# The rest of a rounded weight in plain products: from a VectorE subtraction to an accumulating transfer from GpSimd's queue

## The chip, the cores and the metric

One core of a Trainium2 chip runs the whole program in one launch. The metric is the device time of one execution in microseconds (us); the kernel before takes 2423.59 us, the median of three runs (2423.26 to 2424.36).

## The reference

Two layers of a diffusion backbone on 640 tokens (512 latent tokens, 128 of context) of width 1024. Each layer has a SwiGLU feed-forward block, a mixer (pooling, windowed attention and an order-2 Hyena convolution side by side) and a second feed-forward block, each with a normed and modulated input and a gated residual:

```python
def swiglu(h, wg, wu, wd):
    return (jax.nn.silu(h @ wg) * (h @ wu)) @ wd
...
    h = rmsnorm(x, p['norm'][0]) * (1 + sc1) + sh1
    x = x + 0.5 * g1 * swiglu(h, p['wg'][0], p['wu'][0], p['wd'][0])
    h = rmsnorm(x, p['norm'][1]) * (1 + sc2) + sh2
    u = h @ p['w_in']
...
    mix = jnp.concatenate([y_pool, a, y_hy], axis=-1) @ p['w_out']
    x = x + g2 * mix
```

All inputs are fp32, the feed-forward width is 2816, and w_in, w_out and the three feed-forward matrices are the weights this document speaks of.

## The kernel before, in words

Activations lie with the width on the partitions, 640 tokens in two halves of 320 (`HT`). fp32 products are made of three products of rounded operands: every operand is held as a part `hi`, rounded to the type fp32r, and a rest `lo`, and PE computes hi·hi, hi·lo and lo·hi (`mul`, L331). `split` makes the two: a cast on ACT (L295) and a subtraction on VectorE (L296). Activations are named ahi/alo or hhi/hlo, weights whi/wlo or kwh/kwl.

Weights come from DRAM in blocks of 128 x 512 or 128 x 384 through SP's queue into `raw`, one of `RAWB` = 4 buffers. Three users split them:

- `load_weight` (L298) for plain products: whi and wlo in `WB` = 5 buffers each. `gemm` (L337) takes one block after another and multiplies it with both halves, 24 matmuls for 512 columns. This serves some gate and up columns, the most of the down products and the mixer's products.
- `load_keep` (L312) for products whose weights are used twice, first for half 0 and then for half 1, so that a norm can follow half by half: kwh and kwl in slots of a common pool. It serves the tail of each of three feed-forward blocks (`DNSKEW` = 5 output columns of the down product, two blocks of 512 and 384 alternating, ten blocks a tail), the start of the feed-forward blocks (gate and up of `UPSKEW` = 2 columns), the start of a mixer (w_in, `MIXSKEW` = 4) and its output (w_out).
- `Seven` (L577), Winograd's form of seven products for the other gate and up columns, has its own `part` (L591), which calls `split` on sums of blocks.

Each engine issues in the order that a scheduler has set at build time from priorities and its own costs. Weight loads and their splits get a higher priority by `AHEAD` = 150 and `AHK` = 150, so they stand ahead of the products that take them, as far as buffers allow. The norm's chain passes over several engines: squares on ACT (`sq`, L453) summed on VectorE (L455), a sum over partitions on PE (`tot`), the variance on VectorE (`var`, L480), its power -1/2 on POOL (`rs`, L482), a diagonal matrix on VectorE (`dg`, L499) and its broadcast by PE (`rsb`). VectorE also computes the modulation vectors from big tables (`junk`, L410), 240 instructions in the gaps. POOL does little else than `rs` and some masks.

Of the kernel before, what the change touches and what calls it, by code (L numbers as in the profile page):

```python
# [11 lines left out]
F32 = mybir.dt.float32  # L12
# [3 lines left out]
ALU = mybir.AluOpType  # L16

P = 128
# [64 lines left out]
def make_consts():  # L83
# [22 lines left out]
    def parts(t):  # L106
        """Two parts of few bits each along a new axis after the partitions."""
        t = t.astype(np.float32)
        m, e = np.frexp(t)
        high = np.ldexp(np.round(m * 4096.0) / 4096.0, e).astype(np.float32)  # L110
        return np.stack([high, t - high], axis=1).reshape(P, 512)
# [19 lines left out]
    for ch in range(2):  # L131
        for half in range(2):
            w = (2, 4, 8, 16)[ch * 2 + half]
            rows = slice(64 * half, 64 * half + 64)
# [49 lines left out]
def hybrid_kernel(ctx: ExitStack, tc: tile.TileContext, a, depth=2, fc=22):  # L184
    nc = tc.nc
    V, S, G, DMA = nc.vector, nc.scalar, nc.gpsimd, nc.sync

    class PE:
        """The tensor engine; while fixed is set it issues in the order of this program."""
        last, fixed = None, False  # L190
# [74 lines left out]
    def load_tables(name, h, n, new=slot):  # L265
        """Tables of cosines and sines, each as the two parts that reduced products take."""
        ts = []
        for q in range(n):
            t = new(512, F32R, name="tab")
            DMA.dma_start(out=t.bitcast(F32), in_=a[name][h, q])  # L270
            ts.append(t.rearrange("p (h c f) -> p h c f", h=2, c=2))
        return ts

    def triple(ps, l_, r_, start, stop):
        """One product from three of parts: left and right are pairs of a rounded operand and its rest."""
        for n, (lh, rh) in enumerate(((l_[0], r_[0]), (l_[0], r_[1]), (l_[1], r_[0]))):
            PE.matmul(out=ps, lhsT=lh, rhs=rh, start=(start and n == 0), stop=(stop and n == 2))
# [16 lines left out]
    def split(src, hi, lo):  # L294
        S.copy(out=hi, in_=src)  # L295
        V.tensor_tensor(out=lo, in0=src, in1=hi.bitcast(F32), op=ALU.subtract)  # L296

    def load_weight(src, n):  # L298
        with tc.high_priority(offset=min(AHEAD, tc.cur_priority)):
            raw = wp.tile([P, n], F32, tag="raw", bufs=RAWB, name=nm("raw"))  # L300
            DMA.dma_start(out=raw, in_=src)
            hi = wp.tile([P, n], F32R, tag="whi", bufs=WB, name=nm("whi"))
            lo = wp.tile([P, n], F32R, tag="wlo", bufs=WB, name=nm("wlo"))
            split(raw, hi, lo)
        return hi, lo
# [6 lines left out]
    def load_keep(src, ahead=AHK):  # L312
        out = []
        for k0, k1 in groups(src.shape[-1] // P, 5):
            n = (k1 - k0) * P
            hi, lo = slot(n, F32R, "kwh"), slot(n, F32R, "kwl")
            with tc.high_priority(offset=min(ahead, tc.cur_priority)):
              for j0, j1 in groups(k1 - k0, 4):
                raw = wp.tile([P, (j1 - j0) * P], F32, tag="raw", bufs=RAWB, name=nm("raw"))
                DMA.dma_start(out=raw, in_=src[:, (k0 + j0) * P:(k0 + j1) * P])  # L320
                split(raw, hi[:, j0 * P:j1 * P], lo[:, j0 * P:j1 * P])
            out.append((k0, k1, (hi, lo)))
        return out
# [36 lines left out]

# [1 line left out]
    condT = cp.tile([P, DC, 32], F32, name="condT")  # L362
# [34 lines left out]
    def ada_group(l, g):  # L397
        """Modulation vectors as products of rows of the transposed weights with the condition, summed along them."""
        def load(n):
            raw = wp.tile([P, 1024], F32, tag="araw", bufs=ARAWB, name=nm("araw"))  # L400
            DMA.dma_start(out=raw, in_=a["adat"][l * 9 + g - len(AG0), n])
            ada_raw[l, g, n] = raw

        def step(n):
            raw = ada_raw[l, g, n // 2]
            i, r = n // 2, n % 2
            c, s = i // 2, i % 2
            junk = tp.tile([P, 1024], BF16, tag="junk", bufs=1, name=nm("junk"))
            with tc.issue_after(pace[0]) if pace else nullcontext():
                V.tensor_tensor_reduce(out=junk, in0=raw, in1=condb[:, r], scale=1.0, scalar=bias(l, g)[:, s, c, r:r + 1],  # L410
                                       op0=ALU.mult, op1=ALU.add, accum_out=mods[l][:, g, c, s, r:r + 1])
            if n == 2 * DC - 1:
                done.add((l, g))

        for n in range(2 * DC):
            ada_q.append(((lambda n=n: load(n // 2)) if n % 2 == 0 else None, lambda n=n: step(n)))
# [27 lines left out]

# [1 line left out]
    ssq = [None, None]  # L446
# [11 lines left out]
    class Norm:  # L458
# [77 lines left out]
        def twist(self):  # L536
            """Sums of the quarters of the normed input that the seven products take; yields after each block of rows."""
            B = modv(self.key[0], self.key[2])
# [36 lines left out]

# [1 line left out]
    class Seven:  # L577
        """Gate and up columns of one block as seven products of sums of quarters (Winograd's form of Strassen's
        scheme): rows are gate and up, columns the two halves of the tokens, the inner dimension is cut in the middle."""

# [213 lines left out]

# [1 line left out]
    filt = {}  # L796
# [6 lines left out]
    def sine(ps, n, q, outs):  # L803
        """Both layers at once, one in each half of the partitions."""
        aa, k = slot(n, name="sa"), slot(n, name="sk")
# [60 lines left out]
    class Filter:  # L866
        """The spectra of one layer's filters of one order."""
        W = 256
# [7 lines left out]
        def pair(self, win, src, c0, first=False):  # L876
            """Taps of the forward and the backward filter, their sum and difference, and their magnitudes."""
            w = slot3(1, self.W, name="win")
# [78 lines left out]

# [1 line left out]
    def cmul(z, k, o, prime):  # L959
# [193 lines left out]

# [1 line left out]
    NAMES = ORDER  # L1155
    def mixer(l, cur, nxt):
# [182 lines left out]
        blocks = []  # L1339
# [39 lines left out]
        def stage_a(j):  # L1379
            """Scores and softmax of the two heads that share a query tile; yields after each block of queries."""  # L1380
            qhi, qlo = qhl[j]
            m = [tiny(4, "m", 8) for _ in range(2)]
            ss = [[], []]
            for b in range(4):
                wi, k0, k1, msk, mo, kbs = blocks[b]
# [8 lines left out]
                for kv in range(2):  # L1394
                    s = slot(512, name="sc")
# [138 lines left out]
        def last():  # L1534
            """The first output blocks' products, but for the query tile that comes last."""
            kept.extend(load_keep(a["wout"][l, d, :, 512:1024]) for d in range(4))
            yield
            for d in range(4):
                open_[d] = acc()
                mul(open_[d], kept[d][0][2], 0, 3, 4, ahl, 0)  # L1540
                yield
# [30 lines left out]

# [1 line left out]
    DMA.dma_start(out=craw, in_=a["cond"])  # L1574
# [230 lines left out]
```

## Time and profile before

| | before |
|---|---|
| median of 3 runs | 2423.59 us |
| span of the profiled execution | 2421.6 us |
| PE busy | 2369.5 us, 98% |
| VectorE (DVE) busy | 1922.5 us, 79% |
| ScalarE (ACT) busy | 1096.9 us, 45% |
| GpSimd (POOL) busy | 18.7 us, 1%, 46 instructions |
| hardware DMA queue | 267.75 MB, 34.7% of 16 engines |

The span is that of one execution taken by the profiler, from the first instruction to the last; the metric is some 2.0 us longer. An engine's share is an average over the whole span: a stage can be bound by another engine than the one with the largest share. PE, DVE, ACT, POOL and SP are the engines; PEld is PE's loading of weights and SPq the queue that issues transfers. PEclk is the granted clock of PE, 1.00 being full speed. A name such as kwl<-raw,kwh gives the output and the inputs of an instruction, L296 the line of the kernel.

### The profile page before, as it was taken

What the parts mean: (1) busy time and instruction counts of PE and PEld (TensorE: products, weight loads), DVE (VectorE), ACT (ScalarE), POOL (GpSimd) and SP (SyncE); (2) the same over time, 40 slices, a digit from 0 to 9 for tenths busy, and PEclk for the clock granted to TensorE, in tenths of its full rate; (3) what the DMA queues carried; (4) which work ended last, traced back from release to release, by engine and by line L of the source; (5) the groups of instructions that cost most, each with busy time, mean ns of one, the idle gap of its engine ahead of it and who ended that gap; (6) DMA issues with size and microseconds to landing.
All of it is one profiled execution on the core that took longest, in us unless ns stands there. A gap on an engine that the chain in (4) does not pass through costs nothing.

```text
span 2421.6 us, 41063 instructions
## 1 busy us (share of the span) xinstructions
PE 2369.5 (98%) x15576; PEld 2243.7 (93%) x15576; DVE 1922.5 (79%) x3885; ACT 1096.9 (45%) x2228; POOL 18.7 (1%) x46
## 2 busy tenths in 40 slices
PE   8999999999989999999999999999998999999999
PEld 3799999999877999999999999999987789999999
DVE  7888898858887897998858778785888788567583
ACT  4653353533445553443536435253434556335251
POOL 0000000000000000000000000000000000000000
PEclk9999999999999999999999999999998999999999
DMA  9434444324411334344322433432441122222222
GB/s 330 160 110 136 135 123 156 99 81 158 135 44 43 103 120 142 127 133 150 101 72 95 127 122 108 133 113 84 135 132 63 47 88 77 81 84 78 84 68 90
DMA packets 132645, 270.36 MB, mean 112 GB/s; under 512 B 15002, under 2 KB 24924, under 8 KB 132320
## 3 DMA queue, kind: packets, MB, share of 16 engines
q1 hardware_dynamic: 132448, 267.75, 34.7%
q8 instruction: 122, 2.00, 0.3%
q14 instruction: 75, 0.61, 0.1%
HBM read 259.56 MB, written 8.13 MB: 111 GB/s over the span
## 4 chain that ended last, share of the span: by engine, by line
PE 92%; DVE 4%; issue 1%; ACT 1%; DMA 1%; POOL 0%; SPq 0%; POOLq 0%; DVEq 0%; ACTq 0%
PE mm L205 78%; PE Z L205 5%; PE o L205 1%; PE pt L209 1%; PE yt L205 1%; PE fk L205 1%; PE mx L205 1%; PE ada L205 1%; PE zf L205 1%; DVE junk L410 0%; PE rsb L205 0%; PE pm L205 0%; PE qbc L205 0%; POOL rs L482 0%; DMA ar<-in_ada 0%
## 5 line engine op out<-in xcount | busy, mean ns | idle before, releaser
L295 ACT CAST whi<-raw 128x512 fp32r<-128x512 f32 (+1 forms) x394 | 238.9, 607 | 467.8 <-PE mm L205 432.8
L205 PE MATMUL mm<-hhi,whi 128*128 128x320 f32 x1440 | 447.6, 311 | 2.9 <-ACT u L1218 2.9
L205 PE MATMUL mm<-hhi,wlo 128*128 128x320 f32 x1440 | 445.7, 310 | 0.0
L205 PE MATMUL mm<-hlo,whi 128*128 128x320 f32 x1440 | 445.3, 309 | 0.0
L205 PE MATMUL mm<-ahi,whi 128*128 128x320 f32 x1198 | 370.2, 309 | 0.0
L205 PE MATMUL mm<-alo,whi 128*128 128x320 f32 x1198 | 370.2, 309 | 0.0
L205 PE MATMUL mm<-ahi,wlo 128*128 128x320 f32 x1198 | 370.2, 309 | 0.0
L296 DVE TENSOR_TENSOR wlo<-raw,whi 128x512 fp32r<-128x512 f32 (+1 forms) x394 | 263.0, 671 | 80.8 <-ACT whi L295 78.7
L410 DVE CUSTOM_DVE_ANT_0 junk<-araw,condb,par 128x1024 bf16<-128x1024 f32 x240 | 307.1, 1280 | 5.2 <-DMA araw<-in_adat 4.1
L205 PEld LDWEIGHTS mm<-hhi,whi 128*128 128x128 f32 x1440 | 270.4, 188 | 7.7 <-ACT u L1218 4.5
L205 PEld LDWEIGHTS mm<-hhi,wlo 128*128 128x128 f32 x1440 | 270.5, 188 | 2.3 <-issue 2.3
L205 PEld LDWEIGHTS mm<-hlo,whi 128*128 128x128 f32 x1440 | 270.3, 188 | 1.0 <-issue 0.9
L205 PE MATMUL mm<-thi,whi 128*128 128x320 f32 x864 | 267.0, 309 | 0.0
L205 PE MATMUL mm<-tlo,whi 128*128 128x320 f32 x864 | 267.0, 309 | 0.0
L205 PE MATMUL mm<-thi,wlo 128*128 128x320 f32 x864 | 267.0, 309 | 0.0
L205 PEld LDWEIGHTS mm<-ahi,wlo 128*128 128x128 f32 x1198 | 224.9, 188 | 0.0
L205 PEld LDWEIGHTS mm<-alo,whi 128*128 128x128 f32 x1198 | 224.9, 188 | 0.0
L205 PEld LDWEIGHTS mm<-ahi,whi 128*128 128x128 f32 x1198 | 224.9, 188 | 0.0
L295 ACT CAST whi<-ex 128x512 fp32r<-128x512 f32 x216 | 134.3, 622 | 188.9 <-PE mm L205 177.6
L296 DVE TENSOR_TENSOR wlo<-ex,whi 128x512 fp32r<-128x512 f32 x216 | 149.0, 690 | 34.8 <-ACT whi L295 30.3
L295 ACT CAST whi<-ws 128x512 fp32r<-128x512 f32 x144 | 89.4, 621 | 163.2 <-PE mm L205 124.0
L205 PEld LDWEIGHTS mm<-thi,whi 128*128 128x128 f32 x864 | 162.2, 188 | 0.0
(263 smaller groups left out, 4710.8 us busy)
## 6 DMA issues: line engine op xcount, KB each, us to landing
araw<-in_adat SPq DMA_DIRECT2D x120, 512.0 KB, 3.8
raw<-in_wgu SPq DMA_DIRECT2D x208, 256.0 KB, 2.9
ex<-in_wgu SPq DMA_DIRECT2D x144, 256.0 KB, 2.7
raw<-in_wd SPq DMA_DIRECT2D x128, 256.0 KB, 2.7
raw<-in_win SPq DMA_DIRECT2D x56, 256.0 KB, 3.2
ar<-in_ada SPq DMA_DIRECT2D x48, 256.0 KB, 5.5
raw<-in_wd SPq DMA_DIRECT2D x64, 192.0 KB, 2.5
tab<-in_tfi SPq DMA_DIRECT2D x32, 256.0 KB, 4.1
```

The lines of the kernel that those rows point to most:

```text
L205: cls.order(nc.tensor.matmul(**k))
L209: cls.order(nc.tensor.transpose(**k))
L295: S.copy(out=hi, in_=src)
L296: V.tensor_tensor(out=lo, in0=src, in1=hi.bitcast(F32), op=ALU.subtract)
L410: V.tensor_tensor_reduce(out=junk, in0=raw, in1=condb[:, r], scale=1.0, scalar=bias(l, g)[:, s, c, r:r + 1], op0=ALU.mult, op1=ALU.add, ac ...
```

## The change

Blocks that `load_weight` and `load_keep` load are no longer split by `split` but by a new helper. The cast on ACT stays; a second instruction on ACT writes the negated rounded part into lo; and a transfer from the queue of POOL adds the weights, read once more from DRAM, onto it. `raw` is then read by the cast alone. `Seven` and all splits of activations stay as they were.

```diff
+    def split_weight(src, raw, hi, lo):
+
+        S.copy(out=hi, in_=raw)
+        S.mul(out=lo, in_=hi.bitcast(F32), mul=-1.0)
+        G.dma_start(out=lo, in_=src, accum_op=ALU.add)
...
     def load_weight(src, n):
...
-            split(raw, hi, lo)
+            split_weight(src, raw, hi, lo)
...
     def load_keep(src, ahead=AHK):
...
-                split(raw, hi[:, j0 * P:j1 * P], lo[:, j0 * P:j1 * P])
+                split_weight(src[:, (k0 + j0) * P:(k0 + j1) * P], raw, hi[:, j0 * P:j1 * P], lo[:, j0 * P:j1 * P])
```

Apart from this only docstrings and comments are gone, so that a line after the helper stands six lines lower (L482 is L488). The list of POOL grows from 51 to 395 rows: 344 transfers, 280 of 256 KB and 64 of 192 KB, 86 MB together. VectorE's list falls by 344 rows and ACT's grows by 344. PE's has the same products in a partly different order.

ACT at the first tail (sq are the squares of the columns before, kwh and kwl the kept blocks of the down weights), before:

```order
L453 ACTIVATE sq_5702<-x 128x320
L295 CAST kwh_5705<-raw_5707 128x512
L295 CAST kwh_5711<-raw_5713 128x384
L295 CAST kwh_5717<-raw_5719 128x512
L295 CAST kwh_5723<-raw_5725 128x384
```

and with the change:

```order
L459 ACTIVATE sq_5756<-x 128x320
L300 CAST kwh_5759<-raw_5761 128x512
L301 ACTIVATE kwl_5760<-kwh_5759 128x512
L300 CAST kwh_5766<-raw_5768 128x384
L301 ACTIVATE kwl_5767<-kwh_5766 128x384
L300 CAST kwh_5773<-raw_5775 128x512
L301 ACTIVATE kwl_5774<-kwh_5773 128x512
```

Each cast is now followed by the negated copy of the same block. PE at the same tail, before:

```order
L205 MATMUL mm_5789<-ahi_4696,kwh_5705 128x320 [waits DVE_49,Activation_49]
L205 MATMUL mm_5789<-alo_4697,kwh_5705 128x320
L205 MATMUL mm_5789<-ahi_4696,kwl_5706 128x320 [waits DVE_49]
L205 MATMUL mm_5789<-ahi_4849,kwh_5705 128x320
L205 MATMUL mm_5789<-alo_4850,kwh_5705 128x320
```

and with the change:

```order
L205 MATMUL mm_5857<-ahi_4744,kwh_5759 128x320 [waits DVE_49,Activation_49]
L205 MATMUL mm_5857<-alo_4745,kwh_5759 128x320
L205 MATMUL mm_5883<-ahi_4744,kwh_5773 128x320 [waits DVE_49,PE_49,Activation_49]
L205 MATMUL mm_5883<-alo_4745,kwh_5773 128x320
L205 MATMUL mm_5857<-ahi_4744,kwl_5760 128x320 [waits DMASW6_49]
```

Two products of the next output column are put ahead of the first one that takes a kwl, which now waits on a transfer.

PE at the second feed-forward start (831 us in the trace; hhi and hlo are the normed input, kwh and kwl the kept gate and up weights, tot and rsb the norm's steps), before:

```order
L205 MATMUL tot_9268<-ones,sq_9213 128x1 [waits DVE_49]
L205 MATMUL tot_9268<-ones,sq_9213 128x1 x2
L205 MATMUL mm_9276<-hhi_9140,kwl_8904 128x320
L205 MATMUL mm_9362<-hhi_9102,kwh_9217 128x320 [waits Activation_49]
L205 MATMUL mm_9362<-hlo_9103,kwh_9217 128x320
L205 MATMUL mm_9362<-hhi_9102,kwl_9218 128x320 [waits DVE_49]
L205 MATMUL mm_9362<-hhi_9108,kwh_9217 128x320
L205 MATMUL mm_9362<-hlo_9109,kwh_9217 128x320
L205 MATMUL mm_9362<-hhi_9108,kwl_9218 128x320
L205 MATMUL rsb_9301<-dg_9302,ones 128x128 [waits DVE_49]
```

and with the change:

```order
L205 MATMUL tot_9384<-ones,sq_9325 128x1 [waits DVE_49]
L205 MATMUL tot_9384<-ones,sq_9325 128x1 x2
L205 MATMUL mm_9392<-hhi_9252,kwl_9015 128x320
L205 MATMUL mm_9478<-hhi_9214,kwh_9329 128x320 [waits Activation_49]
L205 MATMUL mm_9478<-hlo_9215,kwh_9329 128x320
L205 MATMUL rsb_9417<-dg_9418,ones 128x128 [waits DVE_49]
L205 MATMUL rsb_9417<-dg_9421,ones 128x128 [waits DVE_49]
L205 MATMUL rsb_9417<-dg_9424,ones 128x64 [waits DVE_49]
L205 MATMUL mm_9503<-hhi_9214,kwh_9343 128x320 [waits PE_49,Activation_49]
L205 MATMUL mm_9503<-hlo_9215,kwh_9343 128x320
L205 MATMUL mm_9531<-hhi_9214,kwh_8993 128x320 [waits Activation_49]
L205 MATMUL mm_9478<-hhi_9214,kwl_9330 128x320 [waits DMASW0_49]
```

The three rsb and three first products of other weights now stand ahead of the first product that takes the new kwl, which waits on a transfer (DMASW0) in place of VectorE.

POOL at the same place with the change; before, its list had the two rs alone there:

```order
L302 DMA kwl_9008<-in_wgu 128x512
L302 DMA kwl_9015<-in_wgu 128x512
L488 TENSOR_TENSOR rs_9160<-var_9158,mhalf 128x3
L488 TENSOR_TENSOR rs_9390<-var_9388,mhalf 128x3
L302 DMA kwl_9330<-in_wgu 128x512
L302 DMA kwl_9337<-in_wgu 128x512
L302 DMA kwl_9344<-in_wgu 128x512
L302 DMA kwl_9351<-in_wgu 128x512
```

The transfers into the last four kept gate and up blocks stand behind both rs of the norm in POOL's list, the first four ahead of them.

PE at the first mixer output (785 us; ahi and alo are the mixer's results, kwh and kwl the kept w_out, pt and o belong to the attention), before:

```order
L205 MATMUL mm_8775<-ahi_8215,kwh_8751 128x320 [waits Activation_49]
L205 MATMUL mm_8775<-alo_8216,kwh_8751 128x320
L205 MATMUL o_8726<-pt_8744,va_6433 64x256
L205 MATMUL mm_8775<-ahi_8215,kwl_8752 128x320 [waits DVE_49]
L205 MATMUL mm_8775<-ahi_8431,kwh_8751 128x320
```

and with the change:

```order
L205 MATMUL mm_8879<-ahi_8311,kwh_8851 128x320 [waits Activation_49]
L205 MATMUL mm_8879<-alo_8312,kwh_8851 128x320
L205 MATMUL o_8826<-pt_8844,va_6505 64x256
L205 MATMUL o_8826<-pt_8849,va_6505 64x256
L209 MATMUL pt_8905<-ident,sc_8595 128x128 [waits PE_49]
L209 MATMUL pt_8905<-ident,sc_8621 128x128
L209 MATMUL pt_8905<-ident,sc_8647 128x128
L205 MATMUL mm_8917<-ahi_8311,kwh_8858 128x320 [waits Activation_49]
L205 MATMUL mm_8917<-alo_8312,kwh_8858 128x320
L205 MATMUL mm_8927<-ahi_8311,kwh_8865 128x320 [waits Activation_49]
L205 MATMUL mm_8927<-alo_8312,kwh_8865 128x320
L205 MATMUL mm_8879<-ahi_8311,kwl_8852 128x320 [waits DMASW4_49]
```

One o, three pt and four products of two later blocks are moved ahead of the first product that takes a kwl.

## Rows read from the trace of the kernel before

**Rows 1.** The page, parts 1 and 3 (DMA: packets, MB, share).
```profile
PE 2369.5 (98%) x15576; PEld 2243.7 (93%) x15576; DVE 1922.5 (79%) x3885; ACT 1096.9 (45%) x2228; POOL 18.7 (1%) x46
...
q1 hardware_dynamic: 132448, 267.75, 34.7%
```

**Rows 2.** PE's waits: line waited for: us in total, times, longest us.
```profile
PE pt L209 <- DVE sc L1351: 7.6, 4, 3.6
PE mm L205 <- ACT kwh L295: 5.8, 3, 2.0
...
PE yt L205 <- DVE cy L969: 2.1, 1, 2.1
...
PE mm L205 <- DVE hlo L533: 1.8, 4, 0.5
PE mm L205 <- DVE kwl L296: 1.7, 4, 0.7
```

**Rows 3.** Timeline, first tail: start us, us, instruction, count [idle before <-releaser].
```profile
509.96 1.16 DVE L296 TENSOR_TENSOR kwl<-raw,kwh 128x512 fp32r<-128x512 f32 x2
...
510.71 0.42 PE L205 MATMUL mm<-ahi,kwl 128*128 128x320 f32 x1 [0.17 <-DVE kwl L296]
```

**Rows 4.** Timeline, first mixer output, VectorE and PE.
```profile
785.51 0.69 DVE L296 TENSOR_TENSOR kwl<-raw,kwh 128x512 fp32r<-128x512 f32 x1 [0.37 <-ACT kwh L295]
...
787.15 0.41 PE L205 MATMUL mm<-ahi,kwl 128*128 128x320 f32 x1
```

**Rows 5.** Timeline, first mixer start, ACT and PE.
```profile
548.24 0.60 ACT L295 CAST kwh<-raw 128x512 fp32r<-128x512 f32 x1
...
553.83 0.41 PE L205 MATMUL mm<-hhi,kwl 128*128 128x320 f32 x1 [0.66 <-DVE kwl L296]
```

**Rows 6.** Timeline, first start of the down products, ACT and PE.
```profile
204.32 0.63 ACT L295 CAST whi<-raw 128x512 fp32r<-128x512 f32 x1
...
211.60 0.31 PE L205 MATMUL mm<-ahi,wlo 128*128 128x320 f32 x1
```

**Rows 7.** Timeline of POOL at the three feed-forward starts.
```profile
831.24 0.85 POOL L482 TENSOR_TENSOR rs<-var,mhalf 128x3 f32<-128x3 f32 x1 [17.99 <-DVE var L480]
...
1269.17 1.24 POOL L482 TENSOR_TENSOR rs<-var,mhalf 128x3 f32<-128x3 f32 x1 [15.48 <-DVE var L480]
...
1990.18 0.85 POOL L482 TENSOR_TENSOR rs<-var,mhalf 128x3 f32<-128x3 f32 x1 [17.97 <-DVE var L480]
```

**Rows 8.** Timeline of PE at the same three places.
```profile
831.34 0.31 PE L205 MATMUL mm<-hhi,kwl 128*128 128x320 f32 x1
...
1271.03 0.39 PE L205 MATMUL mm<-hhi,kwl 128*128 128x320 f32 x1
...
1990.14 0.31 PE L205 MATMUL mm<-hlo,kwh 128*128 128x320 f32 x1
1990.29 0.31 PE L205 MATMUL mm<-hhi,kwl 128*128 128x320 f32 x1
```

**Rows 9.** Groups by shape: count | busy us, mean ns | idle before.
```profile
L295 ACT CAST kwh<-raw 128x512 fp32r<-128x512 f32 x79 | 46.3, 621 | 29.4 <-DMA raw<-in_wd 14.7 <-DMA raw<-in_wgu 9.1 <-DMA raw<-in_win 5.3
...
L410 DVE CUSTOM_DVE_ANT_0 junk<-araw,condb,par 128x1024 bf16<-128x1024 f32 x240 | 307.1, 1280 | 5.2 <-DMA araw<-in_adat 4.1
L296 DVE TENSOR_TENSOR wlo<-raw,whi 128x512 fp32r<-128x512 f32 x345 | 235.7, 687 | 40.8 <-ACT whi L295 39.0
```

**Rows 10.** The page, part 6: DMA issues, count, KB each, us to landing.
```profile
raw<-in_wd SPq DMA_DIRECT2D x128, 256.0 KB, 2.7
...
ar<-in_ada SPq DMA_DIRECT2D x48, 256.0 KB, 5.5
```

**Rows 11.** Windows: us, engines' busy us, PEclk, DMA share, GB/s.
```profile
507.70:509.98 2.28, 0.33 (x4) 0.07 (x2) 1.59 (x5) 1.14 (x4) 0.00 (x0) 1.00 0.00 0
511.60:515.08 3.48, 3.48 (x15) 3.48 (x14) 0.59 (x2) 1.03 (x2) 0.00 (x0) 0.51 0.82 243
711.70:716.40 4.70, 4.68 (x11) 3.11 (x12) 4.70 (x10) 2.52 (x6) 0.00 (x0) 0.50 0.01 3
```

## Prediction

> **What bounds the kernel now.** I first read the busy shares at the head of the page [rows 1]: TensorE is busy for 98% of the span of 2421.6 us, VectorE for 79%. So VectorE's work counts only where PE waits for it, and the change must be judged at the places where PE takes a fresh weight. The profiled execution's 2421.6 us stand beside a median of 2423.59 us; the sum is made against the former, and 2.0 us are added at the end.
>
> Second, PE's waits [rows 2]. The subtraction that the change removes (kwl, L296) held PE up four times, for 1.7 us in all. That is the direct gain at most. Behind the four is the question that decides: how long before PE's first use of a rest is its cast done? I call this the lead. In the steady run of plain products it is longest, since the buffers (WB, RAWB) are filled ahead of PE. I then looked on the timeline for places with a short lead:
>
> - three feed-forward tails (508, 1228, 1667 us): the casts stand behind the sums of squares on ACT, VectorE's first subtraction starts at 509.96 us, as the cast ends, and PE takes its result at 510.71 us [rows 3]. Lead 0.75 us. The others are alike: the row of the waits on kwh counts three, longest 2.0 us [rows 2].
> - two mixer outputs (785, 1945 us): cast done by 785.51 us, PE at 787.15 us [rows 4]: lead 1.6 us.
> - two mixer starts (554, 1712 us): cast done at 548.24 + 0.60 = 548.84 us, PE waits 0.66 us and starts at 553.83 us [rows 5]: lead 5.0 us, so the subtraction stood behind other work of VectorE.
> - twelve starts of down products, the first of them: cast done at 204.32 + 0.63 = 204.95 us, PE at 211.60 us [rows 6]: lead 6.65 us.
> - three feed-forward starts (831, 1271, 1990 us), where the cast was early but, as the order shows, the new transfer is queued on POOL behind `rs`. That ends at 831.24 + 0.85 = 832.09, 1270.41 and 1991.03 us [rows 7]; PE took the first rest at 831.34, 1271.03 and 1990.29 us [rows 8], so before, 0.75 us ahead of rs's end, 0.62 behind it, and 0.74 ahead of it.
>
> **The change part by part.** *Removed:* 344 subtractions on VectorE at 0.69 us for 512 columns [rows 9], 0.55 us for the 64 of 384 columns (by width): some 228 us. VectorE's share falls from 79% to about 70%. PE feels only a part: its waits on VectorE in the mixers (sc 7.6, cy 2.1, hlo 1.8 us [rows 2], 11.5 us) are chains of dependent work, of which I give a third: **-4 us**.
>
> *Added on ACT:* 344 negated copies. Their nearest row is the cast of the same tile, 0.61 us [rows 9], so 210 us on an engine that is 45% busy [rows 1]. Mostly hidden; in the mixers they stand ahead of evictions and exponentials for which PE waits, **+2 us**. If ACT's cover were gone it would be 0.6 us each at the ten places with a short lead.
>
> *Added transfers:* 344, 86 MB, from POOL, into a tile that ACT has just written. They can't be issued before the negated copy is done; the subtraction could run right behind the cast. So the time from cast to usable rest, 0.7 us before, becomes 0.6 us plus a whole transfer. No row shows a transfer from POOL or one that accumulates. The nearest are 256 KB transfers from SP: 2.7 us (raw from in_wd, all along the kernel) and 5.5 us (ar from in_ada, in the crowded first stretch) [rows 10]. Accumulating must also read the destination, and tails are stretches of load; below 2.7 I see no reason to go. I take the middle, **4.1 us**, as my estimate; ends 2.7 and 5.5. Cast to rest is then 0.62 + 4.1 = 4.7 us.
>
> By the Trainium skill, page "DMA: Bandwidth & Descriptors", section "Anatomy of one DMA — SWDGE (gpsimd) path", such a transfer takes about 2.0 us and its bytes over 436 GB/s, 2.6 us here as an estimate; the sum would be about 2436 us by it. No run here shows it.
>
> Place by place, with what PE now has ahead of the rest (as the order shows, 0.147 us for each matmul, which is the step between the last two of [rows 8]):
> - tails: 4.7 - 0.75 - 0.3 (two matmuls put ahead) = 3.65, three times: **+10.9**. The first rest is what counts; the following ones come at ACT's pace, two operations of 0.6 us, under the 12 x 0.147 = 1.8 us that PE takes for 512 columns and one half.
> - feed-forward starts: 832.09 + 4.1 - 831.34 - 0.8 (three rsb and three matmuls put ahead) = 4.05; 1270.41 + 4.1 - 1271.03 - 0.6 = 2.9; 1991.03 + 4.1 - 1990.29 - 0.8 = 4.05: **+11.0**.
> - mixer outputs: 4.7 - 1.6 - 1.8 (one o, three pt and four matmuls put ahead) = 1.3, twice: **+2.6**.
> - mixer starts: 548.84 + 4.7 = 553.54 against 553.83: -0.3, twice: **-0.6**.
> - down starts: 4.7 is under 6.65: **0**. The cover is PE's work on earlier columns; over a transfer of 6 us it is gone, at 12 us for each us.
> - the DMA engines: 267.75 MB took 34.7% of the span [rows 1], so 0.32 MB per us at full load; 0.262 MB take 0.8 us, twice that if the destination is read too. The steady run uses 512 columns in 24 x 0.147 = 3.5 us: **0**.
> - queue of POOL: its 46 instructions before are 18.7 us [rows 1]; `rs` may now stand behind a transfer that waits for ACT. In the order only one of the rs pairs is near one, with a lead: **0**.
>
> *Clock.* A stall of PE can cost twice. After the gap at 507.7 us the granted clock was 0.51 for 3.48 us; after a longer one at 707.8 us it was still 0.50 for 4.70 us after work had come back [rows 11], the lower of the two levels (1.2 against 2.4 GHz). The six stalls of tails and feed-forward starts are of the longer kind (2.9 us and more on top of what there is): 6 x 4.70/2 = 14.1, less 2 x 3.48/2 = 3.5 that two tails pay already: **+10.6**.
>
> Sum: -4 + 2 + 10.9 + 11.0 + 2.6 - 0.6 + 10.6 = +32.5, hence 2454.1 us of span, **2456 us** by the metric. At 2.7 us a transfer (stalls 6.7 and 6.8, none at the outputs, -1.3, clock +3.5 as at the shorter gap, -2) it is +14, 2437 us; at 5.5 (15.2, 15.2, 5.4, +2.3, 10.6, -2) it is +47, 2470 us.
>
> **The rivals.** *B, slow transfers.* If a transfer takes 5.5 to 7.5 us, the down starts lose their cover too: at 7.5 it is 21.2 (tails) + 21.2 (feed-forward starts) + 9.4 + 6.3 (mixers) + 12 x 1.47 (down) + 10.6 - 2 = +84, 2508 us. For it: 5.5 us is a row, and a tail adds ten of them to its own loads. Against: 2.7 us for the 128 transfers of the same weights. One way to it is that a transfer's start waits for whatever VectorE is doing, up to a `junk` of 1.28 us [rows 9], hence 5.4 us and 2469 us. The Trainium skill states a rule of this kind, page "SBUF — State Buffer", section "Who interferes with whom": the descriptors of a GpSimd transfer can't be written while VectorE holds the port they share in a two-port mode. Which of these instructions would hold it no row here shows.
>
> *C, the steady run.* If POOL can't start one transfer per 3.5 us, PE waits at each of 344: at 4.0 us +0.5 x 280 and +1.4 x 64 (2.6 us for 384 columns), some +230, over 2600 us. Against: the byte sum above.
>
> *D, faster.* PE's waits on VectorE vanish with the 228 us of subtractions: sc 7.6, cy 2.1, hlo 1.8 us [rows 2], and half of the 4.70 us at half clock behind one of them [rows 11], -13.9 in all, while a transfer takes only 2.0 us and its stalls cost no clock: 4.7 + 4.7 - 1.3 = +8. That is -6, 2418 us. It decides at about 2.1 us a transfer; above that the stalls (6 us for each us) eat the gain. Against: no 256 KB row is that short, and the chain of sc is its own operations, not a queue of subtractions.
>
> *E, nothing to measure.* The work put ahead of the rests covers them; 2424 us. It needs the moved matmuls to be worth more than I count, or the relief of VectorE and the stalls to cancel, at some 2.5 us a transfer with D's whole gain. That the change doesn't do what it says is out: the order has 344 transfers on POOL.
>
> **How the numbers follow.** Forecast 0.60 (2437 to 2470), B 0.22, C 0.07, D 0.06, E 0.05. The range, 2432 to 2505 us, leaves out C, D and E, 0.18 in all. A difference of 0.2% (4.8 us) is about what a measurement can tell here: faster 0.06, same 0.05, slower 0.89.
>
> **What would show it.** PE should wait on a transfer into kwl for 3 to 4 us at each tail and feed-forward start, eight or ten waits in all, with half clock after six; 344 POOL transfers landing in about 4 us; VectorE near 70%, ACT near 54%; wlo never waited for. Waits on wlo at the down starts speak for B, at every group for C. I am wrong if the kwl waits come to less than 10 us, or if PE's time goes to other places, such as ACT's operations in the mixers.

## The result and the profile after

The changed kernel takes 2511.07 us, the median of three runs (2506.04 to 2513.48), against 2423.59 us: slower, ratio 1.0349 with a 95% interval of 1.0323 to 1.0375. The profiled execution's span went from 2421.6 to 2504.3 us, +82.7 us; +32.5 us were forecast, and the range ended at 2505 us.

The page of the changed kernel, parts 1 and 3 (answering [rows 1]); q0 is the queue of POOL's transfers:

```profile
PE 2399.2 (96%) x15576; PEld 2267.1 (91%) x15576; DVE 1725.3 (69%) x3541; ACT 1290.9 (52%) x2572; POOL 316.3 (13%) x390
...
q1 hardware_dynamic: 132448, 267.75, 33.3%
q0 software_dynamic: 49536, 86.01, 20.9%
```

PE was busy 29.7 us longer with the same 15576 matmuls. By the trace's record of the granted clock it worked for 89.6 us at 0.50 (1.2 GHz), before for 41.5 us; half of the difference, 24 us, is the half clock. It was idle for 2504.3 - 2399.2 = 105.1 us in place of 52.1, +53.0 us. The two make the 82.7 us. VectorE and ACT went to 69% and 52%, as forecast. On q0 86.01 MB took 20.9% of the span, 0.164 MB per us of all 16 engines; on q1 it is 0.321. By the time of its packets an accumulated byte thus costs twice a plain one from SP: 1.6 us of all engines for 256 KB against 0.8. Packets can overlap, so this is no least time for a block: in e9's burst below 256 KB come out at some 1.3 us.

PE's waits in the changed kernel (answering [rows 2]):

```profile
PE mm L205 <- DMA kwl<-in_wout: 15.1, 6, 5.3
PE mm L205 <- DMA kwl<-in_wd: 11.8, 11, 3.4
PE mm L205 <- DMA kwl<-in_wgu: 9.3, 5, 4.5
PE mm L205 <- ACT kwh L300: 8.7, 5, 2.0
...
PE tot L205 <- DVE sq L461: 6.1, 3, 2.9
PE mm L205 <- DVE sq L461: 5.9, 3, 2.0
```

36.2 us on transfers into kwl, where 24.5 had been forecast; no wait on wlo is in the list at all. Beside them stand waits that weren't forecast: kwh from ACT 8.7 us, tot from VectorE 6.1 us (before 1.0). The 5.9 us on sq are the three first products of the tails, which stood under kwh before (5.8 us); so all of the 8.7 us on kwh are new. 9.3 of the 11.8 us on in_wd are the first rests of the three tails (3.41, 2.59 and 3.30 us).

Where the time went, by place. PE issues the same 15576 matmuls in nearly the same order, so the start of the n-th can be compared between the two traces; the growth of that difference over a place is what the place costs, half clock included. The runs of the experiments are set beside it:

| us more than before | changed | e2 | e4 | e8 | e9 | e10 |
|---|---|---|---|---|---|---|
| up to 500 us, with the first feed-forward start | 5.5 | 6.7 | 5.4 | 7.9 | 6.4 | 10.6 |
| 3 tails | 22.9 | 22.7 | 16.6 | 24.0 | 19.8 | 16.4 |
| 2 mixer starts | 7.1 | 7.1 | 5.5 | 7.7 | 10.2 | 7.3 |
| rest of the mixers | 4.1 | -0.4 | 3.0 | 1.7 | 4.9 | 3.6 |
| 2 mixer outputs | 21.1 | 21.0 | 12.2 | 0.5 | 12.4 | 23.5 |
| 3 later feed-forward starts | 21.8 | 21.1 | 19.4 | 22.4 | 15.4 | 22.0 |
| steady run and down starts behind them | 0.0 | 0.0 | 0.0 | 0.0 | 0.0 | 0.6 |

So 78.4 of the 82.5 us lie at the places with a short lead, 4.1 in the rest of the mixers, and none in the steady run. In e10 some 6 us of the first row arise before 60 us, ahead of POOL's first transfer (91.5 us there), so they aren't the change's. How a place looks now, first the tail on the timeline (answering [rows 3]):

```profile
515.50 0.63 ACT L301 ACTIVATE kwl<-kwh 128x512 fp32r<-128x512 f32 x1
...
516.42 0.86 POOL L302 DMA_DIRECT2D kwl<-in_wd  x1 [15.70 <-ACT kwl L301]
...
515.52 0.41 PE L205 MATMUL mm<-ahi,kwh 128*128 128x320 f32 x1 [1.95 <-DVE sq L461]
...
517.65 0.41 PE L205 MATMUL mm<-ahi,kwh 128*128 128x320 f32 x1 [1.57 <-ACT kwh L300]
...
521.72 0.63 PE L205 MATMUL mm<-ahi,kwl 128*128 128x320 f32 x1 [3.41 <-DMA kwl<-in_wd]
```

The transfer is issued 0.3 us behind the negated copy's end (515.50 + 0.63 = 516.13), and PE waits for it 3.41 us. The two products put ahead didn't bridge anything: they wait 1.57 us for their own cast, which is now the third in ACT's list with two copies between. Without that wait PE would have stood before the transfer the longer; the two together are 4.98 us, where 3.65 were forecast.

How long single transfers took, from the rows of L302 in narrow stretches: one at 2086.45 us with no other transfer beside it; one at 211.12 us, the first of POOL's there, but beside SP's plain loads; then the first and the third of the tail, issued at 516.42 and 518.55 us, and the ninth, issued at 528.95 us:

```profile
DMA to landing us min/median/max: 4.1/4.1/4.1
...
DMA to landing us min/median/max: 4.3/4.3/4.3
...
DMA to landing us min/median/max: 5.2/5.2/5.2
...
DMA to landing us min/median/max: 7.3/7.3/7.3
...
DMA to landing us min/median/max: 7.8/7.8/7.8
```

Alone 4.1 us, which was my estimate. In the burst it grows from 5.2 to 7.8 us. The third lands at 525.85, the ninth at 536.75 us: six blocks in 10.9 us, 1.8 us each (by turns 192 and 256 KB). They were also issued 1.73 us apart (518.55 to 528.95), since the plain loads that the casts wait for came late too. The DMA engines were full: their share in a window of this stretch is 1.12 (the last three columns are PEclk, DMA share and GB/s; over 1 means that packets overlap):

```profile
526.00:537.00 11.00, 10.08 (x66) 9.29 (x65) 1.65 (x3) 7.15 (x13) 5.12 (x6) 1.00 1.12 263
```

The groups of the page, part 6 and its continuation (answering [rows 10]), have the medians from issue to landing:

```profile
wlo<-in_wd POOLq DMA_DIRECT2D x113, 256.0 KB, 5.8
raw<-in_win SPq DMA_DIRECT2D x56, 256.0 KB, 6.1
...
kwl<-in_wgu POOLq DMA_DIRECT2D x32, 256.0 KB, 8.2
...
kwl<-in_wout POOLq DMA_DIRECT2D x16, 256.0 KB, 8.1
kwl<-in_wd POOLq DMA_DIRECT2D x15, 256.0 KB, 8.4
```

By the median every kept group (kwl) lands in more than 8 us, and SP's own loads of w_in slowed from 3.2 to 6.1 us. The first mixer output on the timeline (answering [rows 4]):

```profile
806.19 0.86 POOL L302 DMA_DIRECT2D kwl<-in_wout  x1 [43.82 <-PE pt L209]
807.36 0.86 POOL L302 DMA_DIRECT2D kwl<-in_wout  x1 [0.31 <-PE pt L209]
...
813.52 0.64 PE L205 MATMUL mm<-ahi,kwl 128*128 128x320 f32 x1 [5.33 <-DMA kwl<-in_wout]
```

and the same 12 us as a window:

```profile
806.00:818.00 12.00, 6.67 (x31) 5.65 (x31) 4.11 (x8) 4.92 (x10) 3.45 (x4) 0.73 0.95 250
```

Before, the like window from 785 us had:

```profile
785.00:797.00 12.00, 11.39 (x71) 7.99 (x68) 10.61 (x20) 5.97 (x14) 0.00 (x0) 1.00 0.66 221
```

The burst has four transfers, 1.17 us apart at POOL, but the first lands at 813.5 us, 7.3 us after its issue, with the DMA engines 95% busy (before: 66%). PE loses 5.33 us; the clock of this stretch is 0.73, against 1.00 before. The rest of the answers: the down start (answering [rows 6])

```profile
209.54 0.62 ACT L300 CAST whi<-raw 128x512 fp32r<-128x512 f32 x1
...
211.12 0.86 POOL L302 DMA_DIRECT2D wlo<-in_wd  x1 [58.98 <-ACT wlo L301]
...
216.82 0.31 PE L205 MATMUL mm<-ahi,wlo 128*128 128x320 f32 x1
```

has its transfer landed at 211.12 + 4.3 = 215.4 us, 5.2 us behind the cast's end and 1.4 us ahead of PE: the cover of 6.65 us held. The mixer start (answering [rows 5]):

```profile
567.20 1.28 DVE L416 CUSTOM_DVE_ANT_0 junk<-araw,condb,par 128x1024 bf16<-128x1024 f32 x1 [0.81 <-DMA araw<-in_adat]
568.96 0.43 PE L205 MATMUL tot<-ones,sq 128*128 128x1 f32 x2 [2.83 <-DVE sq L461]
```

Here PE waits for VectorE: `junk` waited 0.81 us for its table from DRAM, which came late behind the transfers, and the sum of squares that PE's `tot` takes stands behind `junk` in VectorE's list. The transfer issued at 562.63 us took 6.4 us and landed at 569.1: even without `tot` PE, free since 566.13, would have stood as long before its first kwl. Over the kernel VectorE waited 28.4 us for these tables, 4.1 us before [rows 9]. And the second feed-forward start (answering [rows 7, 8]):

```profile
861.59 0.85 POOL L488 TENSOR_TENSOR rs<-var,mhalf 128x3 f32<-128x3 f32 x1 [17.95 <-DVE var L486]
862.39 0.91 POOL L302 DMA_DIRECT2D kwl<-in_wgu  x1
867.84 0.86 POOL L302 DMA_DIRECT2D kwl<-in_wgu  x1 [4.54 <-ACT hhi L538]
...
864.61 0.45 ACT L538 ACTIVATE hhi<-y,mod 128x192 fp32r<-128x192 f32 x1 [3.68 <-DVE y L523]
...
865.49 0.60 ACT L300 CAST kwh<-raw 128x512 fp32r<-128x512 f32 x1
...
866.14 0.64 PE L205 MATMUL mm<-hhi,kwh 128*128 128x320 f32 x1 [2.02 <-ACT kwh L300]
...
872.02 0.42 PE L205 MATMUL mm<-hhi,kwl 128*128 128x320 f32 x1 [1.90 <-DMA kwl<-in_wgu]
```

The transfer at 862.39 us did go out as `rs` ended, as forecast; but PE's losses are others, though their sum, 2.02 + 1.90 = 3.92 us, is near the 4.05 that were forecast. ACT stood waiting 3.68 us for the norm's y ahead of a copy and a cast, so PE waited 2.02 us for that cast (kwh), and then 1.90 us for a transfer that could only go out at 867.84 us. The first transfer took 4.0 us and landed at 866.4, 0.3 us behind that cast, so it would have held PE as long.

### The profile page after: what moved, and what is told of

The parts are those of the page before. It is cut to its first block, busy times and chain, and to the rows that moved or that the text cites. A ratio compares the mean times of both kernels' runs of the same rounds, so it can differ in the third digit from the quotient of the medians.

```text
span 2504.3 us, 41803 instructions
## 1 busy us (share of the span) xinstructions
PE 2399.2 (96%) x15576; PEld 2267.1 (91%) x15576; DVE 1725.3 (69%) x3541; ACT 1290.9 (52%) x2572; POOL 316.3 (13%) x390
## 3 DMA queue, kind: packets, MB, share of 16 engines
q0 software_dynamic: 49536, 86.01, 20.9%
## 4 chain that ended last, share of the span: by engine, by line
PE 86%; DMA 5%; issue 5%; DVE 2%; ACT 2%; POOL 1%; SPq 0%; POOLq 0%; DVEq 0%; ACTq 0%
PE mm L205 72%; PE Z L205 5%; PE fk L205 1%; PE yt L205 1%; PE zf L205 1%; DMA kwl<-in_wgu 1%; DMA kwl<-in_wd 1%; PE pt L209 1%; DMA kwl<-in_wout 1%; POOL kwl L302 1%; PE o L205 1%; PE mx L205 1%; PE ada L205 1%; DMA tab<-in_tfi 1%; DMA araw<-in_adat 0%
## 5 line engine op out<-in xcount | busy, mean ns | idle before, releaser
L416 DVE CUSTOM_DVE_ANT_0 junk<-araw,condb,par 128x1024 bf16<-128x1024 f32 x240 | 307.2, 1280 | 29.7 <-DMA araw<-in_adat 28.4
L300 ACT CAST whi<-raw 128x512 fp32r<-128x512 f32 x250 | 149.4, 599 | 290.3 <-PE mm L205 265.2
L302 POOL DMA_DIRECT2D wlo<-in_wd x162 | 140.3, 866 | 1121.3 <-ACT wlo L301 1101.2
L572 DVE SCALAR_TENSOR_TENSOR x<-mm,g,x 128x320 f32<-128x320 f32 x96 | 52.8, 550 | 201.9 <-PE mm L205 201.4
```

The costliest lines, as they stand in the source:

```text
L300: S.copy(out=hi, in_=raw)
L302: G.dma_start(out=lo, in_=src, accum_op=ALU.add)
L572: V.scalar_tensor_tensor(out=x[:, d, 0:HT], in0=ps[:, :HT], scalar=g[:, d, 0:1], in1=x[:, d, 0:HT], op0=ALU.mult, op1=ALU.add)
```

## The experiments

The numbers 264 and 80 in the first two expectations (80 again in e8's) were miscounted: 250 plain blocks have a transfer and 94 kept ones. The order of the instructions is set anew for every kernel. Each run stood beside runs of the kernel before on its chip; the ratio is to those.

**e1: the plain products alone.**

```diff
-                split_weight(src[:, (k0 + j0) * P:(k0 + j1) * P], raw, hi[:, j0 * P:j1 * P], lo[:, j0 * P:j1 * P])
+                split(raw, hi[:, j0 * P:j1 * P], lo[:, j0 * P:j1 * P])
```

> load_weight has the accumulating transfer (264 of the 344), load_keep the subtraction of before. Theory K (the whole loss lies at the kept weights, whose rest is wanted a few us after its cast, and the plain products have cover): 2420 to 2426 us, with no wait of PE on a transfer into wlo. Theory T (the sheer number of transfers, their load on the DMA engines or on POOL, costs wherever they run): some 2/3 or more of the loss, 2480 us or more.

Measured: 2429.67 us, ratio 1.0024 (1.0009 to 1.0040). With 250 of the 344 transfers the loss is all but gone: T falls, though the time is 4 us above K's range. No wait on wlo; of the 6 us that stay, most is in the Hyena stages of the two mixers, where two waits like this stand:

```profile
PE yt L205 <- DVE cw L970: 7.5, 2, 3.8
```

**e2: the kept weights alone.**

```diff
-            split_weight(src, raw, hi, lo)
+            split(raw, hi, lo)
```

> load_keep has the accumulating transfer (80 of the 344), load_weight the subtraction. Theory K: 2500 to 2511 us, as with the full change. Theory T: at most 2450 us.

Measured: 2505.65 us, ratio 1.0331 (1.0303 to 1.0359). 94 transfers, 24 MB, carry the loss: K holds.

**e3: no transfer.**

```diff
         S.mul(out=lo, in_=hi.bitcast(F32), mul=-1.0)
-        G.dma_start(out=lo, in_=src, accum_op=ALU.add)
```

> As the changed kernel, without the transfer: lo stays the negated rounded part, so the rest is left out of the weights and only the work on ACT and its order are left. Theory L (the loss is the time that a transfer takes to land, and the half clock after the waits): 2415 to 2430 us. Theory A (the 344 instructions added to ACT and the changed orders cost by themselves, as the late kwh casts and the longer waits on DVE sq, cy and cw in the mixers suggest): 2440 us or more.

Measured: 2433.30 us, ratio 1.0026 (1.0013 to 1.0039), a span of 2424.9 us. ACT's 344 instructions, the new orders and the relief of VectorE together cost some 6 us. That is 3 us above L's range and 7 below A's, so L holds in the main. But the order isn't quite the changed kernel's: PE's waits on kwh are 5.9 us in all here, those of the tails alone, so e5 has to tell what ACT's order is worth.

**e4: no accumulation.**

```diff
-        G.dma_start(out=lo, in_=src, accum_op=ALU.add)
+        G.dma_start(out=lo, in_=src)
```

> The same transfers from POOL, without accumulating: lo then holds the weight itself in place of its rest. Theory Q (the accumulation makes the transfers slow: in the changed kernel a byte of the POOL queue took twice the engine time of one of SP's queue): kwl lands in about 4 to 5 us from its issue in place of 8, the time is 2440 to 2465 us. Theory P (POOL's issue at 0.86 us each and the fixed part are what is slow): kwl still lands in 7 us or more, 2490 us or more.

Measured: 2485.49 us, ratio 1.0253 (1.0220 to 1.0286); between the two theories. Landings of kept blocks in this run:

```profile
kwl<-in_wgu POOLq DMA_DIRECT2D x32, 256.0 KB, 5.4
...
kwl<-in_wout POOLq DMA_DIRECT2D x16, 256.0 KB, 6.3
```

against 8.2 and 8.1 us. The first lands somewhat later than Q had it, and the time is above Q's range. So the accumulation is worth some 2 to 3 us of the landing and 20.5 us of the span (2504.3 to 2483.8), and a plain transfer from POOL would still lose 62 us.

**e5: the negated copy on VectorE.**

```diff
-        S.mul(out=lo, in_=hi.bitcast(F32), mul=-1.0)
+        V.tensor_scalar(out=lo, in0=hi.bitcast(F32), scalar1=-1.0, scalar2=None, op0=ALU.mult)
```

> The negated copy is made by VectorE in place of ACT, all else as changed; VectorE then has its 344 instructions back. Theory A (in ACT's list the copies stand ahead of casts and of the normed inputs, and that is why kwh is late): PE's waits on kwh fall from 8.7 us to about 6, rsb and kwh at the feed-forward starts come earlier, 2490 to 2500 us. Theory L (only the landing counts): 2505 to 2515 us.

Measured: 2511.85 us, ratio 1.0362 (1.0346 to 1.0377). The waits on kwh are gone from the head of the list, as A had it, but nothing is won: PE waits for the transfers instead, now at the mixer starts (in_win) too:

```profile
PE mm L205 <- DMA kwl<-in_wout: 20.5, 6, 7.8
...
PE mm L205 <- DMA kwl<-in_win: 13.1, 2, 6.9
```

What ACT's order cost was hidden behind the landing. A falls. VectorE has its 344 instructions back here, so the two effects aren't told apart at the mixer starts.

**e6: without the loads of the modulation tables.**

```diff
-            raw = wp.tile([P, 1024], F32, tag="araw", bufs=ARAWB, name=nm("araw"))
-            DMA.dma_start(out=raw, in_=a["adat"][l * 9 + g - len(AG0), n])
+            if len(araws) < ARAWB:
+                raw = wp.tile([P, 1024], F32, tag="araw", bufs=ARAWB, name=nm("araw"))
+                DMA.dma_start(out=raw, in_=a["adat"][l * 9 + g - len(AG0), n])
+                araws.append(raw)
+            raw = araws[n % ARAWB]
```

> The modulation tables are loaded into their two buffers once and used again, so 118 loads of 512 KB are left out and most modulation vectors are not computed from their own weights. Theory C (the transfers at the mixer outputs and starts are slow because they share the DMA engines with these loads): kwl lands in about 6 us in place of 8.2, the mixer outputs cost 5 us each in place of 10, in all 2490 to 2500 us. Theory B (they are slow by themselves, four in a row that each take twice their time): kwl in 7.5 us or more, 2503 us or more.

Measured: 2500.80 us, ratio 1.0317 (1.0299 to 1.0334), too near to the changed kernel's ratio to tell them apart by time. The landings fall only a little:

```profile
PE tot L205 <- DVE sq L464: 3.9, 2, 1.9
...
kwl<-in_wout POOLq DMA_DIRECT2D x16, 256.0 KB, 7.6
```

The mixer outputs cost 17.6 us in place of 21.1, the mixer starts 2.8 us in place of 7.1. But `tot` still waits 1.9 us at both starts, with no table to come late, where the changed kernel has 2.8 and 2.9: only about 1 us of that wait is the table's. The trace has no half clock at e6's mixer starts, and the changed kernel has it at both, 6.4 us of PE's time in all; so most of what the starts gain is the clock. Nearer to B than to C.

**e7: the plain products of the feed-forward blocks alone.**

```diff
-                split_weight(src[:, (k0 + j0) * P:(k0 + j1) * P], raw, hi[:, j0 * P:j1 * P], lo[:, j0 * P:j1 * P])
+                split(raw, hi[:, j0 * P:j1 * P], lo[:, j0 * P:j1 * P])
...
     def gemm_steps(src, rhs, ps):
...
-            wt = load_weight(src[:, k0 * P:k1 * P], (k1 - k0) * P)
+            wt = load_weight(src[:, k0 * P:k1 * P], (k1 - k0) * P, False)
```

(With False `load_weight` takes the subtraction.)

> Only the plain products of the feed-forward blocks have the transfer (about 200 of the 344); the mixers' products and all kept weights are subtracted on VectorE, and PE's list is that of the kernel before. Theory K: 2423 to 2426 us, the same as before: the relief of VectorE is worth nothing and the transfers cost nothing there. If the relief is worth something: 2418 us or less. If the plain products of the mixers were not the cause of the 6 us that stayed in the first experiment: 2429 us.

Measured: 2426.12 us, ratio 1.0009 (0.9999 to 1.0020): no difference. VectorE's share is down from 79% to 75%, PE's busy time is 2369.2 us as it was. So the relief is worth nothing, and the transfers cost nothing where the lead is long.

**e8: the kept w_out subtracted.**

```diff
-            kept.extend(load_keep(a["wout"][l, d, :, 512:1024]) for d in range(4))
+            kept.extend(load_keep(a["wout"][l, d, :, 512:1024], new=False) for d in range(4))
```

(The same for the other four; with new=False `load_keep` takes the subtraction.)

> As the changed kernel, with the subtraction on VectorE for the kept w_out alone (16 of the 80 kept blocks). Theory K by places (each place costs by itself; the two mixer outputs 10 to 11 us each): 2488 to 2492 us. If the waits move on to the next place (the feed-forward start right behind): 2500 us or more.

Measured: 2485.87 us, ratio 1.0256 (1.0240 to 1.0271), a little better than expected. The outputs cost 0.5 us in place of 21.1 and the feed-forward starts behind them the same as ever: each place costs by itself.

**e9: kept blocks without their plain load.** The cast reads a tile that is always there, so that lo takes up what hi lacks.

```diff
-                raw = wp.tile([P, (j1 - j0) * P], F32, tag="raw", bufs=RAWB, name=nm("raw"))
-                DMA.dma_start(out=raw, in_=src[:, (k0 + j0) * P:(k0 + j1) * P])
+                raw = condb[:, 0, :(j1 - j0) * P]
```

> The kept blocks are cast from a tile that is always there in place of their own weights, so SP's 94 loads into raw for them are left out and their rounded parts are wrong; the 94 accumulating transfers stay. Theory S (in a burst the DMA engines are the limit: each block costs a plain load and an accumulating transfer, about 0.8 + 1.6 us of all 16 engines, so the blocks land 1.9 to 2.5 us apart and the first lands late): the spacing in a tail falls from 1.9 to at most 1.7 us, kwl lands in 5.5 to 7 us in place of 8.4, 2475 to 2495 us. Theory P (a transfer is slow by itself, or POOL's pace sets it): kwl still in 8 us, 2503 us or more.

Measured: 2492.72 us, ratio 1.0276 (1.0259 to 1.0294). In the first tail the transfers issued at 517.47, 519.64 and 524.80 us took, from the rows of L302 (the second row takes in one at 519.09, and its larger time is that of 519.64):

```profile
DMA to landing us min/median/max: 4.6/4.6/4.6
...
DMA to landing us min/median/max: 5.5/5.9/6.2
...
DMA to landing us min/median/max: 6.6/6.6/6.6
```

The third of the burst (519.64) lands at 525.8, five blocks later one (524.80) at 531.4 us: 1.1 us each, issued 1.03 us apart, where the changed kernel had 1.8 and 1.73. The medians:

```profile
kwl<-in_wout POOLq DMA_DIRECT2D x16, 256.0 KB, 5.4
kwl<-in_wd POOLq DMA_DIRECT2D x15, 256.0 KB, 6.2
```

in place of 8.1 and 8.4 us. S holds in the landings: with the plain loads gone they come 2 us sooner and nearer to each other. Two things go together here: the DMA engines have less to move, and the casts no longer wait for a load. The five blocks are three of 192 KB and two of 256, 1.11 MB in 5.5 us or 0.20 MB per us; 256 KB thus take some 1.3 us of the engines, not the 1.6 that S counted, and with a plain load of 0.8 us the six blocks of the changed kernel's tail would take 11.0 us, where 10.9 were measured. The loss is not gone, since the first transfer's 4.6 us are still several times the lead.

**e10: the first of each group subtracted.**

```diff
-        return [[load_keep(a["wgu"][l, i, f, w], ahead) for w in range(2)] for f in range(n)]
+        return [[load_keep(a["wgu"][l, i, f, w], ahead, f + w > 0) for w in range(2)] for f in range(n)]
```

(The same for w_in, w_out and the down weights.)

> As the changed kernel, with the subtraction on VectorE for the first output column of every group of kept weights (22 of the 94 kept blocks), the transfer for the others. Theory F (my step that the first rest alone counts, the following ones have ACT's pace and cover): most of the loss is gone, at most 2450 us. Theory S (the blocks behind it wait too, since they land about 2 us apart and 7 to 8 us after their issue): 2465 to 2495 us, with PE still waiting on kwl for 15 us or more.

Measured: 2507.23 us, ratio 1.0332 (1.0313 to 1.0350); slower than S had it, and far from F. The waits moved to the next column:

```profile
PE mm L205 <- DMA kwl<-in_wout: 16.4, 6, 3.5
PE mm L205 <- DMA kwl<-in_wd: 10.7, 8, 3.1
PE mm L205 <- DMA kwl<-in_wgu: 9.1, 6, 4.5
```

36.2 us in all, by chance the very sum of the changed kernel. Only the tails gained (16.4 in place of 22.9 us).

## Why the prediction was right in sign and wrong in size

- **Right: where.** The places with a short lead are those that lose, and the steady run and the down starts lose 0.0 us. e1, e2 and e7 show it. By place the 50 us that the forecast lacks are 18.5 at the mixer outputs, 8.5 at the tails, 7.7 at the mixer starts, 5.5 at the first feed-forward start, 3.7 at the later ones and 6.1 in the rest of the mixers.
- **Right, by luck: the lone transfer.** 4.1 us taken, 4.1 measured at 2086.45 us. The figure was the middle between two rows of plain loads from SP, and no row was of this kind. The Trainium skill's page "DMA: Bandwidth & Descriptors", section "Anatomy of one DMA — SWDGE (gpsimd) path", gives 2.6 us for these bytes, as an estimate from its figures; a plain transfer of e4 with no other beside it (2065.93 us) took 2.9 us, near to that, and the accumulating one is 1.5 us above it.
- **Wrong, the step that failed: "the DMA engines ... twice that if the destination is read too ... 0".** I set the average load of the span, one block per 3.5 us, against 1.6 us. At the short leads blocks come in bursts at ACT's and POOL's pace, 1.2 us, each with its plain load; together they take 1.8 us at the tail, by the landings there. The engines were 95% busy at the output, the landing went from 4.1 to 8.4 us (median of the tails), and e9 undid 2 us of it by taking the plain loads out. The same transfer time for a lone block and for the fourth of a burst was the error.
- **Wrong: "The first rest is what counts; the following ones come at ACT's pace".** At the tails the first rest does make 9.3 of the 11.8 us. But the following ones land 1.8 us apart, and 5 to 8 us after their issue, so they have no cover of their own: e10 took the first column out of it and PE waited 36.2 us as before.
- **Mixer outputs: +2.6 forecast, 21.1 measured.** Both errors together: the four products, one o and three pt put ahead were worth what I counted, but the landing was 7.3 us (the two first waits were 5.33 and 4.89 us), and each output has a second burst of four, which cost another 2.4 to 2.5 us. Some 5 us are the half clock behind the waits. e8 shows that it is the kept w_out's transfers and nothing behind them.
- **Tails: +10.9 and about 3.5 of the clock, 22.9 measured;** feed-forward starts +11.0 and 7, 21.8 measured. At the tails the landing was 5.2 us in place of 4.1. The feed-forward starts are nearest to the mark, though only in part for the reason given: `rs` did hold the first transfer up, but the trace puts 2.02 us to a late cast (kwh) in ACT's list, which ended just ahead of the landing, and 1.90 us to a second transfer that ACT's list held up.
- **Mixer starts: -0.6, measured 7.1.** The lead of 5.0 us was too short for a landing of 6.4 us, though the trace puts the wait to `tot`, which comes first in PE's list. I also named no one who shares the DMA engines with the transfer: VectorE's tables came late, which e6 shows to be about 1 us of that wait.
- **First feed-forward start: 0, measured 5.5.** I had looked only at the later three. e3, without a transfer, has about 1.5 of it.
- **Clock: +10.6, measured 24** of the 29.7 us by which PE's busy time grew. The six stalls that I counted made 11.4 of it, as forecast; the mixer starts and outputs, which I had left out, made another 11.4, and the window of the output shows 0.73 over 12 us.
- **VectorE's relief: -4, and ACT: +2.** e7 has the relief at nothing; e3 has both with the new orders at about +6.
- **Rival B** had the number (2508 us), and its reason, that a tail adds ten transfers to its own loads, is the one that the runs bear out: the kept blocks landed in 7.3 to 8.4 us. But 17.6 us of its sum were the down starts' cover, which they kept, so that the number came out is in part luck. Its other way, that a transfer's start waits for VectorE, isn't seen: POOL's issuing instructions in the steady run took the same whatever VectorE did (rows of L302, ns min/median/max):

```profile
L302 POOL DMA_DIRECT2D wlo<-in_wd x162: 862/865/893, 211.1 to 2486.5; - x162
```

The Trainium skill's rule on the page "SBUF — State Buffer", section "Who interferes with whom", speaks of two-port modes; these 162 instructions, with VectorE busy for 69% of the span, show no stall of that kind, though no row tells whether any of VectorE's instructions was in such a mode, and a lock on the part of the work after the issue isn't told apart here.

What stays open: why e1 keeps 6 us, when the feed-forward part of it costs nothing. It loses 6.1 us in the rest of the mixers, where e3, with the same copies and no transfer, is 3.8 us faster than before; so the copies alone aren't the cause, but whether the transfers delay cw or the order does isn't told apart. Open is also how much of e4's 62 us is its landing of 5 to 6 us and how much the half clock that follows.

## What to carry to other kernels

Before an operation is moved from an engine to a transfer, ask at each place how long the result may take from the last input to its first use; an average engine share says nothing about it. Price the transfer as it comes at that place, in its burst with all that loads there at the same time, and ask whose loads it delays. A busy engine off the critical path is no reason to relieve it: 4 points off VectorE's share were worth nothing here (e7).

## What the runs showed of the hardware

By the time of their packets, accumulating transfers from POOL moved 0.164 MB per us of all 16 engines against 0.321 for SP's plain ones and, in e4, 86.01 MB in 13.0% of 2483.8 us, 0.266, for POOL's plain ones. Its issue held POOL for 0.86 us; without accumulation (e4, rows of L302, ns min/median/max) it is

```profile
L302 POOL DMA_DIRECT2D wlo<-in_wd x162: 530/530/553, 211.3 to 2465.9; - x162
```

So accumulating cost about 0.33 us more of POOL and 1.6 times the packet time of a plain transfer on the same queue. With no other transfer beside it, 256 KB landed in 4.1 us accumulating and in 2.9 us plain. In e9's burst accumulated blocks moved at 0.20 MB per us: the packets' time overstates what a block needs.
